# One ring of raw slots for single units and pairs, and three more panels with a second seven

## The chip, the cores and the metric

One NeuronCore of a Trainium2 chip runs the whole program. The metric is the device time of one execution in microseconds (us). Its engines work side by side, each on its own queue of instructions: PE (TensorE, matmuls), DVE (VectorE), ACT (ScalarE), POOL (GpSimd) and SP (SyncE, which here only issues transfers). Semaphores hold an instruction, and all that is queued behind it on its engine, until what it needs is there.

## The reference, cut to what matters

A decoder trunk of two layers on 256 tokens of width 2048, in float32. Layer 0 mixes tokens by gated linear attention, layer 1 by forgetting attention; both also attend to 256 memory tokens. Behind each stands a channel mixer, and only this is touched here:

```
def conv_ffn(h, w_up, conv_w, conv_b, w_down):
    u = causal_dwconv(h @ w_up, conv_w, conv_b)
    a, val = split_cols(u, [FFN_HIDDEN, FFN_HIDDEN])
    return (jax.nn.silu(a) * val) @ w_down
...
    h = rmsnorm(x, norm_ffn[i])
    x = x + conv_ffn(h, ffn_w_up[i], ffn_conv_w[i], ffn_conv_b[i], ffn_w_down[i])
```

`w_up` is 2048 x 11264 and `w_down` 5632 x 2048, so the weights are read once and used for 256 tokens. A causal convolution of width 3 along the tokens lies between.

## The kernel before, in words

**Precision.** TensorE multiplies in a rounded float32 form. Each float32 number is therefore carried in two parts, hi (rounded) and lo (what is left), and a product is made of three matmuls: hi x hi, lo x hi, hi x lo. Activations are split once. Weights are split as they arrive: ACT casts a raw tile to `whi` and DVE subtracts to get `wlo`. Both have five buffers.

**Units, panels, turns.** The weights lie in memory in the order of use, in units of at most 128 x 1024 numbers (512 KB). A panel is the units of one set of columns. `split_unit` (L211) loads one unit into a buffer `raw` (five buffers, tag "raw", on the right side of memory), casts and subtracts; `split_apart` (L195) does the same into smaller tiles. Ahead of the first mixer 20 panels of 8 units are loaded; a mixer has 264 units; between the mixers stand 7 panels of 8, 8 of 4 and 4 of 8 units.

**A channel mixer** (`ffn`, L1403) has 11 up panels of 16 units, numbered here 0 to 10, and three parts of down panels, of 16, 12 and 16 rows of blocks. The order is up panels 0 to 4, the two down panels of the first part, up panels 5 to 7, the two of the second, up panels 8 to 10, the third part (one panel of 16 joint units, then two of 8 narrow units). In code a panel is named by j, four times its number. `m` is a ring of 20 chunks of the gated product, which is why parts of down follow so early.

**Pairs and sevens** (`pair_steps`, L388). An up or joint down panel works on two halves of tokens by two halves of columns. A single unit k takes 4 places x 3 = 12 matmuls of 512 columns (L413). Two neighbouring units are a 2 x 2 block product; with sums of the two chunks of tokens at hand (`usum`, `dsum`) and sums of the two units of weights, seven block products do instead of eight: 21 matmuls instead of 24. This costs DVE four sums over half units (L438 to L441) in the raw tiles, and four casts and four subtractions (`split_more`, L376, instructions at L383 and L384): w1 and w2 of the raw units, w3 and w4 of the sums. The two units of a pair go to special tiles, `raw2`, two buffers in the pool that the mixer is given, and their loads (L432) are queued behind the last load issued. All up panels do this with units 6 and 7 (`SEVEN_UP`); panels in `MORE_IN` also with units 11 and 12 (`SEVEN_MORE`). In those panels the first pair comes after four single units, not six, three singles stand between the pairs, and five follow. The token sums for both pairs are made in every mixer (`input_sums`). Four of the joint down panels' pairs also go as sevens (`SEVEN_DOWN`).

**Order.** Instructions are ordered by a planner at build time: by priority (loads, casts and subtractions run ahead by `AHEAD`), by what they wait for, and by hand-written edges (`issue_after`). While a panel runs, the panel before is finished: its columns are turned by a trip through memory (L651, L656 on POOL), and taps, silu and gating are dealt out unit by unit (`tick`), in panels of `MORE_IN` with a larger share (1.7, not 1.45), and one unit earlier for the first half of the panel in front of one.

**The pools.** In layer 0 the mixer's pool is `turn1`. It is opened when the linear attention's pools `near` and `gla` close; in `near` lie the blocks (`blk`) that the norm ahead of the mixer sends through memory (`preparing`, L1596). In layer 1 the mixer's pool is `store`, opened when `turn2` closes, which holds only that norm's blocks. The block of the last 512 columns is sent (`far<-blk`) when the output projection `wo` in front of the mixer has ended. At the end of the first mixer the four blocks of the next norm are written: 0 and 1 in the `raw2` buffers, 2 and 3 in those of `dsum`.

Of the kernel before, what the change touches and what calls it, by code (L numbers as in the profile page):

```python
# [13 lines left out]
F32 = mybir.dt.float32  # L14
# [6 lines left out]
P = 128  # L21
# [13 lines left out]
SEVEN_UP = (6,)  # L35
SEVEN_DOWN = {4: 0, 10: 1, 20: 0, 34: 1}
SEVEN_MORE = 11
MORE_IN = (2, 5, 6, 8, 9)
SCRATCH = 4096


LEVELS = (64, 16, 4)
# [2 lines left out]
NUNIT = 1024  # L45
# [102 lines left out]
def _trunk(ctx: ExitStack, tc: tile.TileContext, xt, xtok, memt, wp, wgu, gns, gfin, cnv, par, msk, out):  # L148
    nc = tc.nc
    where, _ = _layout()  # L150
# [4 lines left out]
    rear = ctx.enter_context(tc.tile_pool(name="rear", bufs=1, side="right"))  # L155
# [28 lines left out]
            TE.matmul(warm, bufB[KC - 1][:, 0, :P], bufB[KC - 1], start=i == 0, stop=i == WARM - 1)  # L184

    loads, casts, lows, ends, last_mm, sent = [], [], [], [], [], []
    scratch = [sm]
    parked = []

# [5 lines left out]
    def split_apart(unit, spare):  # L195

        off, kcs, n = unit
        w = len(kcs) * n
        with tc.high_priority(offset=AHEAD):
            raw = rear.tile([P, NUNIT], F32, name="raw", tag="raw", bufs=5)  # L200
            loads.append(nc.sync.dma_start(raw[:, :w], wp[off : off + P * w].rearrange("(p n) -> p n", p=P)))
            hi, lo = [], []
            for j in range(len(kcs)):
                s = slice(j * n, (j + 1) * n)
                hi.append(spare())
                lo.append(spare())
                casts.append(S.activation(hi[j], raw[:, s], AF.Copy))
                lows.append(V.tensor_tensor(lo[j], raw[:, s], hi[j].bitcast(F32), ALU.subtract))
        return hi, lo

    def split_unit(unit, pieces=1, before=None, between=int):  # L211

        off, kcs, n = unit
        w = len(kcs) * n
        with tc.high_priority(offset=AHEAD):
            raw = rear.tile([P, NUNIT], F32, name="raw", tag="raw", bufs=5)
            hi = wpool.tile([P, NUNIT], F32R, name="whi", tag="whi", bufs=5)
            lo = wpool.tile([P, NUNIT], F32R, name="wlo", tag="wlo", bufs=5)
            src = wp[off : off + P * w].rearrange("(p n) -> p n", p=P)
            for i in range(pieces):  # L220
                s = slice(i * w // pieces, (i + 1) * w // pieces)
                if i:
                    between()
                loads.append(nc.sync.dma_start(raw[:, s], src[:, s]))
            if n % P:
                a, b, c = (t.rearrange("p (j m) -> p j m", j=len(kcs))[:, :, :n] for t in (raw[:, :w], hi, lo))
                casts.append(S.activation(b, a, AF.Copy))
                lows.append(V.tensor_tensor(c, a, b.bitcast(F32), ALU.subtract))
                return hi, lo
            for i in range(pieces):  # L230
                s = slice(i * w // pieces, (i + 1) * w // pieces)
                if before is not None:
                    before(i)
                casts.append(S.activation(hi[:, s], raw[:, s], AF.Copy))  # L234
                lows.append(V.tensor_tensor(lo[:, s], raw[:, s], hi[:, s].bitcast(F32), ALU.subtract))  # L235
        return hi, lo
# [150 lines left out]
    def pair_steps(units, src, sums, flip, pool, early, late, ahead=0):  # L387
# [38 lines left out]
        for k in plan:  # L426
            if k in sums:
                with tc.high_priority(offset=AHEAD):
                    ra, rb = [pool.tile([P, NUNIT], F32, name="raw2", tag="raw2", bufs=2) for _ in range(2)]
                    with tc.issue_after(loads[-1].ins):  # L430
                        for t, (off, _, w) in ((ra, units[k]), (rb, units[k + 1])):
                            loads.append(nc.sync.dma_start(t, wp[off : off + P * w].rearrange("(p n) -> p n", p=P)))  # L432
                st = [[sums[k][:, part, j, :] for part in range(2)] for j in (3, 0, 1, 2)]
                done = k == end[-1]
                w1 = split_more(ra[:, :512], 512)
                w2 = split_more(rb, 1024)
                with tc.high_priority(offset=AHEAD):
                    V.tensor_tensor(ra[:, :512], ra[:, 512:], ra[:, :512], ALU.subtract)  # L438
                    V.tensor_tensor(ra[:, 512:], rb[:, 512:], ra[:, 512:], ALU.subtract)  # L439
                    V.tensor_tensor(rb[:, 512:], rb[:, 512:], ra[:, :512], ALU.subtract)  # L440
                    summed = V.tensor_tensor(rb[:, :512], rb[:, :512], rb[:, 512:], ALU.subtract)  # L441
                three("p1", tok(k, 0), [t[:, :512] for t in w1], done)
                three("p2", tok(k + 1, 0), [t[:, :512] for t in w2])
                three("p3", st[3], [t[:, 512:] for t in w2])
                with tc.issue_after(summed.ins):
                    w3 = split_more(ra, 1024)
                three("p5", st[0], [t[:, :512] for t in w3], done)
                three("p7", st[2], [t[:, 512:] for t in w3], done)
                w4 = split_more(rb, 1024)
                three("p6", st[1], [t[:, 512:] for t in w4], done)  # L450
                last_mm.append(three("p4", tok(k + 1, 1), [t[:, :512] for t in w4]))
                if done:
                    with tc.issue_after(casts[-1].ins), tc.issue_after(lows[-1].ins):
                        early(bank)
                yield -1
                yield -1
                continue
            else:
                w = split_unit(units[k])
                last = k == n - 1  # L460
                steps = [(low, *place) for low in range(2) for place in places]
                if last:
                    steps.sort(key=lambda t: places.index(t[1:]))
                for low, name, b, h in steps:
                    for part in range(2 - low):
                        r = mm(name, tok(k, b)[part], w[low][:, h * 512 : (h + 1) * 512], last and low == 1)
                    if last and low:
                        ends.append(r)
                        late(b, h, bank[name])
                last_mm.append(r)  # L470
            yield k
# [923 lines left out]
    def ffn(l, nx, h, m, ys, zs, landing, then, pool, temps, last=None, spare=None):  # L1395
        with tc.tile_pool(name=f"ffn{l}", bufs=1) as fp:
            def held(name, i):
                return pool.tile([P, 2, 4, P], F32R, name=name, tag=f"{name}{i}")

            up_sums = {k: held("usum", k) for k in (*SEVEN_UP, SEVEN_MORE)}  # L1400
            rooms = {i: held("dsum", i) for i in range(2)}
            cw = fp.tile([P, 4 * 88], F32, name="cw")
            nc.sync.dma_start(cw, cnv[l])  # L1403
            taps = [fp.tile([P, 2, 2, T + i], F32, name=f"tap{i}") for i in range(3)]
# [89 lines left out]
            def up_pair(j):  # L1494

                count[2] += 1
                second = j // 4 in MORE_IN
                turns = [turn(j + 2 * h_, 7 if not h_ and j // 4 + 1 in MORE_IN else 8) for h_ in range(2)]
                u = {}
# [31 lines left out]
            def drive_up(j):  # L1531
                drive(up_pair(j), 1.7 if j // 4 in MORE_IN else 1.45)

# [27 lines left out]
            if l:  # L1561
                f2, f3 = [rows_tm(("down", l, p, f), src, evac) for f, evac in ((2, third), (3, last))]
            else:
                for f, k in ((2, 0), (3, 1)):
                    then.rooms[f] = lambda k=k: pool.tile([P, 4, 4, 2, 32], F32, name="tblk", tag=f"dsum{k}")
                f2 = panel_tm(("down", l, p, 2), src, third)
                f3 = panel_tm(("down", l, p, 3), src, lambda b, a: (add_to(3)(b, a), then(3, b)))
            last_pair = hi - lo - 4
# [9 lines left out]
            if l:  # L1578
                for u in range(3, 8):
                    f2(u)  # L1580
                for u in range(4):
                    f3(u)
                for b in range(2):
                    for u in range(4, 8):
                        f3(u, (b,), spare if u < 6 else None)
            else:
                hooks = {(2, 3): then.land, (2, 5): then.land, (2, 7): then.take, (3, 1): then.take, (3, 2): then.land,
                         (3, 5): then.take}
                for f, step, at in ((2, f2, 3), (3, f3, 0)):
                    for u in range(at, 8):  # L1590
                        step(u)
                        hooks.get((f, u), int)()

    def preparing(name, dst, pool, far, kept=None, tag="blk", queue=nc.sync):

# [43 lines left out]
    with tc.tile_pool(name="stash", bufs=1) as st:  # L1639
# [4 lines left out]
        with tc.tile_pool(name="turn1", bufs=1) as tp:  # L1644
            n2, then = preparing("kv", bufB, tp, dram, turned3, "raw2", nc.gpsimd)
# [13 lines left out]
    with tc.tile_pool(name="turn2", bufs=1) as tp:  # L1659
        n, then = preparing("ffn1", bufA, tp, dram)  # L1660
# [139 lines left out]
```

## Time and profile before

| | |
|---|---|
| median of 3 runs (lowest, highest) | 2210.38 us (2208.87, 2210.74) |
| the profiled execution | 2211.01 us |
| its span, first to last instruction | 2209.2 us |
| granted TensorE clock, mean | 0.998 |
| DVE, ACT busy | 82%, 65% of the span |
| read from memory | 469.62 MB |
| first mixer begins, second begins (first matmul of L413) | 456.9, 1493.7 us |

The page has the share of the span in which each engine was busy, the chain of work that ended last, and groups of instructions by line. In a row of a group stand line, engine, operation, output<-inputs and count; then busy time, mean ns of one, and what ended the engine's idle time in front of them. A row of the timeline has start, length, engine, line, operation, names and count, and in brackets the idle time in front of it and what released it.

### The profile page before, as it was taken

The numbers are of one execution on the slowest core, as the hardware profiler recorded it, in microseconds if no ns is written. First come the engines' busy times: TensorE is split into PE (matmuls) and PEld (weight loads), VectorE is DVE, ScalarE is ACT, GpSimd is POOL, SyncE is SP. The second block draws the span as 40 slices with busy tenths as digits, with TensorE's granted clock in tenths as the row PEclk, the third lists the DMA queues.
The fourth block names the chain that finished last, engine by engine and source line by source line (L and its number), as shares of the span: only waits on it lengthen the run. The fifth ranks groups of instructions, "written<-read, shape, count | busy, mean of one in ns | idle before, by whom it ended". The sixth has DMA issues, their size and how long they took to land.

```text
span 2209.2 us, 30105 instructions
## 1 busy us (share of the span) xinstructions
PE 2197.2 (99%) x10303; PEld 1849.1 (84%) x10303; DVE 1804.7 (82%) x2679; ACT 1426.7 (65%) x2268; POOL 137.2 (6%) x257
## 2 busy tenths in 40 slices
PE   9999999999999999999999999999999999999998
PEld 7888888888888888888888998888888888888886
DVE  7768976688998888889877669668898888888996
ACT  6655655556787568657865555455788657765774
POOL 0000000001100010001110000000100000100010
PEclk9999999999999999999999999999999999999999
DMA  9777677867778567666778767776677757676673
GB/s 367 253 223 220 192 209 225 256 219 249 235 248 267 189 212 248 229 232 221 247 252 259 227 201 244 228 240 231 227 239 236 254 184 247 228 266 206 223 271 131
DMA packets 166291, 515.42 MB, mean 233 GB/s; under 512 B 20780, under 2 KB 42552, under 8 KB 166136
## 3 DMA queue, kind: packets, MB, share of 16 engines
q1 hardware_dynamic: 149064, 460.99, 63.1%
q0 software_dynamic: 16496, 51.71, 7.4%
q8 instruction: 81, 1.33, 0.2%
q10 hardware_dynamic: 576, 0.79, 0.1%
q14 instruction: 74, 0.61, 0.1%
HBM read 469.62 MB, written 43.79 MB: 232 GB/s over the span
## 4 chain that ended last, share of the span: by engine, by line
PE 99%; DVE 0%; ACT 0%; issue 0%; DVEq 0%; ACTq 0%
PE acc L413 29%; PE acc L339 26%; PE ps_s L413 15%; PE ps_o L413 8%; PE ps_t L413 7%; PE acc L310 3%; PE acc L265 3%; PE ps_s L339 2%; PE acc L369 2%; PE acc L263 1%; PE ps_s L1036 0%; PE ps_o L702 0%; PE ps_s L702 0%; PE ps_s L1309 0%; PE ps_s L1082 0%; PE ps_o L1264 0%
## 5 line engine op out<-in xcount | busy, mean ns | idle before, releaser
L235 DVE TENSOR_TENSOR wlo<-raw,whi 128x1024 fp32r<-128x1024 f32 (+2 forms) x697 | 828.0, 1201 | 235.3 <-ACT whi L234 214.4
L234 ACT ACTIVATE whi<-raw 128x1024 fp32r<-128x1024 f32 (+2 forms) x697 | 717.6, 1046 | 356.1 <-PE acc L339 135.2
L339 PE MATMUL acc<-whi,B 128*128 128x512 f32 (+3 forms) x1248 | 290.9, 369 | 0.0
L383 ACT ACTIVATE whi<-raw 128x1024 fp32r<-128x1024 f32 (+1 forms) x160 | 151.9, 954 | 197.1 <-DVE raw L439 64.5
L339 PEld LDWEIGHTS acc<-whi,B 128*128 128x128 f32 x1248 | 226.8, 188 | 28.1
L384 DVE TENSOR_TENSOR wlo<-raw,whi 128x1024 fp32r<-128x1024 f32 (+1 forms) x160 | 173.4, 1085 | 25.9 <-ACT whi L383 23.5
L413 PE MATMUL acc<-whi,mix 128*128 128x512 f32 x750 | 191.9, 389 | 0.0
L413 PE MATMUL acc<-whi,B 128*128 128x512 f32 x728 | 188.4, 389 | 0.0
L413 PEld LDWEIGHTS acc<-whi,mix 128*128 128x128 f32 x750 | 140.8, 188 | 29.3
L413 PEld LDWEIGHTS acc<-whi,B 128*128 128x128 f32 x728 | 136.6, 188 | 28.4
L339 PE MATMUL acc<-wlo,B 128*128 128x512 f32 (+3 forms) x624 | 159.1, 369 | 0.0
L339 PEld LDWEIGHTS acc<-wlo,B 128*128 128x128 f32 x624 | 114.2, 188 | 14.6
L1415 ACT ACTIVATE tap<-yzu,cw 128x256 f32<-128x256 f32 x264 | 121.2, 534 | 2.6 <-DVE wlo L235 1.9
L1415 ACT ACTIVATE tap<-fvt,cw 128x256 f32<-128x256 f32 x264 | 121.2, 534 | 0.3 <-DMA fvt<-far 0.3
L1422 DVE TENSOR_TENSOR tap<-tap,tap 128x1024 f32<-128x1024 f32 x88 | 106.7, 1213 | 5.9 <-ACT tap L1415 5.9
L413 PE MATMUL acc<-wlo,mix 128*128 128x512 f32 x375 | 105.6, 389 | 0.0
L413 PE MATMUL ps_s<-whi,mix 128*128 128x512 f32 x382 | 105.1, 389 | 0.0
L413 PE MATMUL acc<-wlo,B 128*128 128x512 f32 x364 | 104.6, 389 | 0.0
L413 PE MATMUL ps_s<-whi,B 128*128 128x512 f32 x336 | 92.1, 389 | 0.0
L413 PEld LDWEIGHTS ps_s<-whi,mix 128*128 128x128 f32 x382 | 71.7, 188 | 14.9
L413 PEld LDWEIGHTS acc<-wlo,mix 128*128 128x128 f32 x375 | 70.4, 188 | 14.6
L413 PEld LDWEIGHTS acc<-wlo,B 128*128 128x128 f32 x364 | 68.3, 188 | 14.2
(502 smaller groups left out, 3890.2 us busy)
## 6 DMA issues: line engine op xcount, KB each, us to landing
raw<-wp SPq DMA_DIRECT2D x741, 512.0 KB, 4.7
fvt<-far POOLq DMA_DIRECT2D x100, 128.0 KB, 3.9
raw<-wp SPq DMA_DIRECT2D x32, 384.0 KB, 3.5
far<-yu POOLq DMA_DIRECT2D x22, 512.0 KB, 3.7
far<-yzu POOLq DMA_DIRECT2D x22, 512.0 KB, 4.3
yzu<-far POOLq DMA_DIRECT2D x88, 128.0 KB, 4.3
raw<-wp SPq DMA_DIRECT2D x24, 388.0 KB, 3.7
x<-xtok SPq DMA_DIRECT2D x8, 512.0 KB, 7.3
```

The source lines that it names most:

```text
L234: casts.append(S.activation(hi[:, s], raw[:, s], AF.Copy))
L235: lows.append(V.tensor_tensor(lo[:, s], raw[:, s], hi[:, s].bitcast(F32), ALU.subtract))
L263: mm = TE.matmul(acc[p][c][:, :T], w[:, s], both[:, 0, :], start=False, stop=end and j == 3)
L265: mm = TE.matmul(acc[p][c], w[:, s], both, start=u == j == 0, stop=end and j == 3)
L310: mm = TE.matmul(acc[b][:, :n], src[kcs[j] - base][:, part, b * P : (b + 1) * P], w, start=u == 0 and low == part == j == 0, stop=u == end ...
L339: mm = TE.matmul(acc[b][:, :n], src[kc - base][:, part, b * P : (b + 1) * P], ready[low][:, j * room : j * room + n], start=i == low == pa ...
L369: mm = TE.matmul(acc[b][:, :n], src[kc - base][:, part, b * P : (b + 1) * P], w, start=i == low == part == j == 0, stop=i == end and low = ...
L383: casts.append(S.activation(hi[:, :n], src, AF.Copy))
L384: lows.append(V.tensor_tensor(lo[:, :n], src, hi[:, :n].bitcast(F32), ALU.subtract))
L413: r = TE.matmul(bank[name], x, w, start=name not in begun, stop=last)
L1415: S.activation(by_run(taps[i][:, s, c, i:]), zs[slot][:, :, 2 * c + s], AF.Copy if i else AF.Identity, bias=0.0 if i else w[3], scale=w[2 ...
L1422: V.tensor_tensor(taps[0], taps[0], taps[n][:, :, :, :T], ALU.add)
```

## The change: one ring, and MORE_IN of eight panels

The five raw buffers become one tile `home`, cut into five slots; `raw_slot()` counts its calls in `taken` and returns slot number `taken % len(slots)`. While a mixer runs, a tile `guest` in the mixer's pool adds two slots, numbers 5 and 6, so that seven are turned; at the mixer's end they are taken off again. Both units of a pair take slots of this ring, in turn with the single units. `MORE_IN` grows from five panels to eight (1, 7 and 10 are new). The four blocks at the end of the first mixer go to the buffers of the two `usum` and the two `dsum`.

```
-MORE_IN = (2, 5, 6, 8, 9)
+MORE_IN = (1, 2, 5, 6, 7, 8, 9, 10)
+RAWS = 5
...
+    home = rear.tile([P, RAWS * NUNIT], F32, name="raw")
+    slots, taken = [home[:, i * NUNIT : (i + 1) * NUNIT] for i in range(RAWS)], [0]
+
+    def raw_slot():
+
+        taken[0] += 1
+        return slots[taken[0] % len(slots)]
...
-            raw = rear.tile([P, NUNIT], F32, name="raw", tag="raw", bufs=5)
+            raw = raw_slot()
...
-                    ra, rb = [pool.tile([P, NUNIT], F32, name="raw2", tag="raw2", bufs=2) for _ in range(2)]
+                    ra, rb = raw_slot(), raw_slot()
...
             rooms = {i: held("dsum", i) for i in range(2)}
+            guest = pool.tile([P, 2 * NUNIT], F32, name="raw2")
+            slots.extend(guest[:, i * NUNIT : (i + 1) * NUNIT] for i in range(2))
...
-                for f, k in ((2, 0), (3, 1)):
-                    then.rooms[f] = lambda k=k: pool.tile([P, 4, 4, 2, 32], F32, name="tblk", tag=f"dsum{k}")
+                for f, tag in enumerate((f"usum{SEVEN_UP[0]}", f"usum{SEVEN_MORE}", "dsum0", "dsum1")):
+                    then.rooms[f] = lambda tag=tag: pool.tile([P, 4, 4, 2, 32], F32, name="tblk", tag=tag)
...
+            del slots[RAWS:]
```

The line with `raw_slot()` stands twice, in `split_apart` and in `split_unit`.

More of the change, by code (lines that the diff above doesn't have):

```diff
@@ L215, in split_unit @@
         with tc.high_priority(offset=AHEAD):
-            raw = rear.tile([P, NUNIT], F32, name="raw", tag="raw", bufs=5)
+            raw = raw_slot()
             hi = wpool.tile([P, NUNIT], F32R, name="whi", tag="whi", bufs=5)
```

## The prediction

> **What bounds the kernel now.** I read the page first: span, busy shares, the chain that ended last.
>
> ```profile
> span 2209.2 us, 30105 instructions
> PE 2197.2 (99%) x10303; PEld 1849.1 (84%) x10303; DVE 1804.7 (82%) x2679; ACT 1426.7 (65%) x2268; POOL 137.2 (6%) x257
> PE 99%; DVE 0%; ACT 0%; issue 0%; DVEq 0%; ACTq 0%
> ```
>
> TensorE is the chain, from end to end. So each matmul that goes is worth its spacing, and each new wait of TensorE is paid in full; DVE, at 82%, is paid only where it hands a weight over late. The timeline of PE in an up panel gives the spacing:
>
> ```profile
> 801.21 1.98 PE L413 MATMUL acc<-whi,B 128*128 128x512 f32 x8
> 803.02 1.07 PE L413 MATMUL acc<-wlo,B 128*128 128x512 f32 x4
> 803.93 1.98 PE L413 MATMUL acc<-whi,B 128*128 128x512 f32 x8
> ```
>
> Twelve matmuls, a single unit, run from 801.21 to 803.93: 2.72 us, 0.2267 us each.
>
> The sum is made against the profiled execution, 2211.0 us (span 2209.2 and 1.8 around it); the median of the runs, 2210.4, lies 0.6 under it. This kernel's measurement tells about 0.2% (4.4 us) from no change.
>
> **The matmuls that go: -4.1 us.** A pair in the long form takes 2 x 12 = 24 matmuls, as a seven 7 x 3 = 21. Three more panels in each of two mixers save 2 x 3 x 3 = 18 matmuls: 18 x 0.2267 = 4.1 us. No operation is added to TensorE. Bytes from memory stay the same.
>
> **DVE's share of a new pair.** Its price, by the groups of lines:
>
> ```profile
> L235 DVE TENSOR_TENSOR wlo<-raw,whi 128x1024 fp32r<-128x1024 f32 (+2 forms) x697 | 828.0, 1201 | 235.3 <-ACT whi L234 214.4 <-PE acc L339 5.1 <-issue 3.1
> L384 DVE TENSOR_TENSOR wlo<-raw,whi 128x1024 fp32r<-128x1024 f32 (+1 forms) x160 | 173.4, 1085 | 25.9 <-ACT whi L383 23.5
> L441 DVE TENSOR_TENSOR raw<-raw 128x512 f32<-128x512 f32 x40 | 27.6, 691 | 1.0
> L438 DVE TENSOR_TENSOR raw<-raw 128x512 f32<-128x512 f32 x40 | 27.2, 681 | 0.6
> ```
>
> A seven costs DVE 173.4 / 40 = 4.34 us of subtractions and four weight sums (L438 to L441) of 0.68 to 0.69, 2.74: 7.08 us. Two singles cost 2 x 1.20 = 2.40. So each new pair adds 4.68 us to DVE while TensorE's panel gets 0.68 shorter. Is there room? Windows on panels 1, 2, 7, 10 and the last joint down panel of the first mixer (start:end, length, then PE, PEld, DVE, ACT, POOL busy):
>
> ```profile
> 499.60:542.50 42.90, 42.90 (x191) 35.50 (x190) 35.09 (x41) 33.40 (x53) 5.47 (x10) 1.00 0.77 261
> 542.50:584.70 42.20, 42.20 (x187) 34.80 (x186) 38.91 (x45) 29.76 (x46) 5.49 (x10) 1.00 0.66 202
> 840.40:883.30 42.90, 42.90 (x191) 35.51 (x190) 36.53 (x47) 34.03 (x56) 5.52 (x10) 1.00 0.75 244
> 1032.20:1075.00 42.80, 42.80 (x190) 35.45 (x189) 36.46 (x47) 33.97 (x56) 5.49 (x10) 1.00 0.76 252
> 1075.00:1118.00 43.00, 42.71 (x189) 35.02 (x188) 41.78 (x51) 30.89 (x50) 5.50 (x10) 1.00 0.73 238
> ```
>
> DVE would be busy 39.8 of 42.2 in panel 1, 41.2 of 42.2 in panel 7, 41.1 of 42.1 in panel 10. It fits on the mean, with a microsecond over. What can be lost is local: panel 2 and the down panel take over a smaller lead. In panel 2's second pair the last cast and its matmul already stand 0.08 us apart:
>
> ```profile
> 554.93 1.61 SPq L432 DMA_DIRECT2D raw<-wp  x2
> 563.82 1.06 ACT L383 ACTIVATE whi<-raw 128x1024 fp32r<-128x1024 f32 x1 [2.10 <-DMA raw<-wp]
> 568.31 1.06 ACT L383 ACTIVATE whi<-raw 128x1024 fp32r<-128x1024 f32 x1 [0.39 <-PE acc L413]
> 569.45 0.71 PE L413 MATMUL ps_t<-whi,usum 128*128 128x512 f32 x2
> ```
>
> The same rows show what the ring repairs: this pair's loads left only at 554.93, when the first pair gave back the two special tiles, and ACT waited 2.10 us for them. With seven slots turned in one ring the second pair's slots are those of the units two and three places ahead of the first pair, so that wait goes. Against it: panel 1 leaves 4.68 + 0.68 = 5.4 us less lead, of which about half its 7.8 idle us (3.9) takes up its part and the vanished wait 2.1. Bounds per mixer: nothing lost, or one whole 4.68. I take 1.5 (about 0.5 at panel 2, 1.0 at the down panel behind panel 10, where DVE has 1.2 us free), since the idle rows lie nearer to the lower end: **+3.0** for both, bounds 0 and 9.4. TensorE has no wait in these panels that could be won back.
>
> **The start of each mixer, where the ring reaches the guest tile: the large term.** Before, the first six singles use the five old slots; the two special tiles are first touched by the pair of unit 6. The pool they lie in takes over memory of a pool that closes just then, the one with the norm's blocks (near, then turn2). SP and ACT at both starts:
>
> ```profile
> 461.47 0.33 SPq L651 DMA_DIRECT2D far<-blk  x1
> 466.26 0.80 SPq L432 DMA_DIRECT2D raw<-wp  x2
> 1498.23 1.10 SPq L651 DMA_DIRECT2D far<-blk  x1
> 1504.01 0.80 SPq L432 DMA_DIRECT2D raw<-wp  x2
> 1504.07 0.63 ACT L688 ACTIVATE usum<-cv 128x512 fp32r<-128x512 f32 x1 [1.90 <-DMA far<-blk]
> 469.55 0.63 ACT L383 ACTIVATE whi<-raw 128x512 fp32r<-128x512 f32 x1 [2.57 <-DMA raw<-wp]
> 471.08 1.06 ACT L383 ACTIVATE whi<-raw 128x1024 fp32r<-128x1024 f32 x1 [0.90 <-DMA raw<-wp]
> ```
>
> Twice the first load into the special tiles leaves at the moment at which the last block's transfer has landed (ACT's write to usum, a tile of the same pool, names that transfer). The guest is allocated in the same pool; I take it that its first write waits for the same thing. Now count calls of the ring. Ahead of the first mixer: 20 panels of 8 units, 160. The mixer: 264. Between: 7 panels of 8, 8 of 4, 4 of 8, 120. So the second mixer begins with call 545, and 545 mod 7 = 6: **its very first unit goes into the guest's second half.** The first mixer begins with call 161, slot 0; its unit 5 and the pair's first half get slots 5 and 6.
>
> *Second mixer.* Unit 0's load now leaves at 1504.0. From issue to landing the first pair's took 469.55 - 466.26 = 3.3 us; the cast takes 1.06: hi is ready at 1508.4. TensorE wants it here:
>
> ```profile
> 1493.66 1.07 PE L413 MATMUL acc<-whi,mix 128*128 128x512 f32 x4
> 1514.08 0.74 PE L413 MATMUL ps_t<-whi,usum 128*128 128x512 f32 x2 [0.94 <-ACT whi L383]
> ```
>
> That is a stall of 14.7 us. Unit 0 opens the accumulators, so nothing of the mixer can go ahead of it; wo is done. Behind the waiting load stand, on SP, the pair's loads and the returns of the norm's blocks; on ACT and DVE the casts of units 1 to 5, whose loads use the five old slots and can have landed: all of that runs faster than TensorE's 2.72 us a unit, and the pair's old stall of 0.94 disappears in the gained lead. Net **+13.8**. Bounds: 0 if the guest's memory is free earlier, 14.7 if nothing is won back.
>
> TensorE then restarts from idle. What that costs, by the kernel's first matmuls, and the granted clock behind its last ones (0.62 is the last but two columns):
>
> ```profile
> 1.46 3.36 PE L184 MATMUL ps_o<-B 128*128 128x512 f32 x7 [1.46 <-DVE B L181]
> 4.71 2.08 PE L310 MATMUL acc<-whi,A 128*128 128x512 f32 x4
> 6.58 1.02 PE L310 MATMUL acc<-wlo,A 128*128 128x512 f32 x2
> 7.43 1.09 PE L310 MATMUL acc<-whi,A 128*128 128x512 f32 x4
> 2200.00:2209.00 9.00, 0.23 (x1) 0.00 (x0) 3.50 (x12) 1.83 (x6) 0.00 (x0) 0.62 0.58 185
> ```
>
> Thirteen matmuls took 7.43 - 1.46 = 5.97 us instead of 2.95, and within 9 us of the end the clock had fallen to a mean of 0.62. So a stop of 14.7 us should cost a second ramp: **+3.0**, bounds 0 and 3.0. The Trainium skill (TensorE: Matmul & The Clock Gate, Part 1) has the array fall to half rate after an idle window of about 3.4 us and come back after as long a busy one; at half rate that would lose an estimated 1.7 us, and the sum would be 1.3 lower. The ramp in these rows, 5.97 us, is longer than that.
>
> *First mixer.* Call 161 gets the slot of call 160, but unit 0 is wanted only at 470.50 - 5 x 2.72 = 456.9. DVE lets go of unit 160 here:
>
> ```profile
> 443.69 1.22 DVE L235 TENSOR_TENSOR wlo<-raw,whi 128x1024 fp32r<-128x1024 f32 x1 [0.88 <-ACT whi L234]
> 470.50 1.98 PE L413 MATMUL acc<-whi,B 128*128 128x512 f32 x8
> 475.04 1.06 ACT L383 ACTIVATE whi<-raw 128x1024 fp32r<-128x1024 f32 x1 [1.52 <-PE acc L413]
> 476.17 0.72 PE L413 MATMUL ps_t<-whi,usum 128*128 128x512 f32 x2
> ```
>
> 444.9 + 3.3 + 1.06 = 449.3: hidden with 7.6 us over; without that cover it would cost the 4.4. Unit 5 leaves at 466.3 and is cast by 470.6, where TensorE wants it at 470.50; the pair's loads fall one place back, 471.08 - 469.55 = 1.5 us, and its last cast stands 0.07 us ahead of its matmul. So about **+1.6**, bounds 0 and 2.5.
>
> **What costs nothing.** The first layer's norm blocks 0 and 1 move from the special tiles to the input sums' tiles: those are read last by panel 10's pair, one down panel (43 us) earlier; were that gone, a DVE transpose would wait. The earlier taps and the larger share in front of and in the new panels move the same instructions by one unit; POOL's transfers keep their places. Leaving a mixer, the ring's next slot is that of five calls back (calls 425 and 420), as before.
>
> **Sum:** -4.1 + 3.0 + 13.8 + 3.0 + 1.6 = +17.3. 2211.0 + 17.3 = 2228.3, less 0.6 for the median: **2228 us**, slower.
>
> **Rivals.**
> *The guest is free in time* (not slower). For it: the new pool is larger than the one that it follows, and its guest may lie on other memory than the blocks. Against: two tiles of that pool, usum and the special ones, both waited. Then only -4.1 + 3.0 is left: 2209.9, by the median 2209, within 0.2%; it decides if the guest may be written before about 1488. With nothing lost in the panels it is 2206.3.
> *DVE becomes the bound*: the 4.68 us of panels 1 and 10 are lost whole, at panel 2 and at the down panel, in both mixers, on top of the starts: 2211.0 - 4.1 + 18.4 + 18.7 = 2244. For it: 0.08 us of lead there. Against: 3.3 idle us in panel 2's window.
> *The slots are not told apart*, as they are now parts of one tile: each load would wait for the unit before, 4.7 us (the page's landing) + 1.05 + 1.20 = 6.95 a unit, 808 units, 5,600 us. Against: the taps' tiles are already written in parts.
>
> **Chances.** Forecast 0.85 (two tiles in two places against one argument); guest free 0.10; DVE bound 0.03; not told apart 0.02. The range takes the forecast's terms from their low ends (clock, panels and first mixer at nothing: 2220.7; 4 us less if the last block leaves earlier) to their high ends (panels 9.4: 2234.7, and one more unit late): 2216 to 2238, some 8 in 10. Faster 0.03 and same 0.07 are the free guest's; slower 0.90.
>
> **What would show it.** Right: 5814 matmuls on L413; PE idle of about 15 us at 1494, its first L413 whi late, released by ACT, ACT by a load; the guest's first load behind far<-blk; matmul spacing of 0.45 for some microseconds behind it. In panel 2 ACT no longer waits 2 us for the second pair. Wrong: unit 0 of the second mixer loaded before 1488, or PE waits in panels 2, 7 and 10 of more than 5 us a mixer.

## The result, and the profile after

The changed kernel takes 2220.79 us (median of 5 runs, 2219.84 to 2221.95); the kernel before took 2210.52 beside it (5 runs, 2208.87 to 2210.86). The ratio is 1.0048, with a 95% interval of 1.0033 to 1.0062: slower by 10.3 us, inside the range and 7.2 us under the forecast of 2228. The profiled execution took 2219.84 us, 8.8 more than that of before, so its trace shows 8.8 of the 10.3 us.

In the new kernel the lines have moved down: the matmul of the mixers is L421 (it was L413), that of `wo` L347 (L339), the cast of a single unit L242 (L234), the casts and subtractions of a pair L391 and L392, a single unit's load L232, a pair's L440, `far<-blk` L659. The page, in the lines that were shown of before (span, busy time, the chain), and one of its groups:

```profile
span 2218.0 us, 30190 instructions
PE 2196.9 (99%) x10285; PEld 1846.7 (83%) x10285; DVE 1828.6 (82%) x2715; ACT 1437.8 (65%) x2280; POOL 136.8 (6%) x257
PE 96%; DVE 2%; ACT 1%; DMA 1%; issue 0%; SPq 0%; DVEq 0%; ACTq 0%
L421 PE MATMUL acc<-whi,mix 128*128 128x512 f32 x746 | 191.7, 392 | 8.7 <-ACT whi L242 8.7
```

TensorE has 18 matmuls fewer (10285 for 10303), and the chain that ended last, wholly TensorE's before, now runs for a few per cent through other engines and a DMA. The last line names the place: one group of matmuls waited 8.7 us for the cast of a single unit. The chain of waits, in order of time (start, length, what), shows what that cast waited for:

```profile
1479.83 12.48 PE acc L347 x55
...
1493.77 0.62 DVE x L507
...
1494.42 0.72 DVE blk L1637
...
1495.16 2.57 DMA far<-blk
1497.73 0.02 SPq L232
...
1497.78 3.42 DMA raw<-wp
...
1501.28 1.06 ACT whi L242
...
1502.39 19.11 PE acc L421 x72
```

Read it downwards: `wo` ends, its last block is added to x and transposed, the block goes to memory, and only when that transfer has landed does the load of the mixer's unit 0 leave, at 1497.78. The timeline of PE at that place, with the standstill in brackets:

```profile
1502.39 3.78 PE L421 MATMUL acc<-whi,mix 128*128 128x512 f32 x8 [8.73 <-ACT whi L242]
1505.97 1.89 PE L421 MATMUL acc<-wlo,mix 128*128 128x512 f32 x4
1507.68 2.03 PE L421 MATMUL acc<-whi,mix 128*128 128x512 f32 x8
1509.55 1.07 PE L421 MATMUL acc<-wlo,mix 128*128 128x512 f32 x4
```

After the stop of 8.73 us twelve matmuls take 1507.68 - 1502.39 = 5.29 us, where 2.72 is the usual; from 1507.68 on the usual pace is back. The granted clock, the last figure but two in the row of a window, was 0.50 from shortly after TensorE stopped until then, and 1.00 on both sides of it:

```profile
1497.50:1507.70 10.20, 5.31 (x13) 4.15 (x14) 6.02 (x6) 7.05 (x11) 0.00 (x0) 0.50 0.56 184
```

The account of the 8.99 us by which the last matmul starts later (2199.84 before, 2208.83 after), all from the starts of TensorE's matmuls (the stop of 8.73 us is counted from the end of the last matmul, so it is a little more here):

| | predicted | measured |
|---|---|---|
| 18 matmuls that go | -4.1 | -4.08 |
| first mixer, its first pair | +1.6 | +1.58 |
| new pairs, panels 7 and 10 of the first mixer, 2, 7 and 10 of the second (the pair in panel 2 had lost 0.11 before) | +3.0 | +1.67 - 0.11 |
| from the end of the first mixer to the start of the second | +14.7 | +8.90 |
| slow matmuls behind that stop | +3.0 | +2.63 |
| the old stall of the second mixer's first pair | -0.94 | -1.34 |
| ahead of the first mixer | none | -0.24 |
| sum | +17.3 | +9.0 |

The predicted worry about DVE is answered by the same windows as before (DVE's busy time is the third figure that has a count behind it), on panels 1, 2, 7, 10 and the last joint down panel of the first mixer:

```profile
501.20:543.40 42.20, 42.20 (x188) 34.95 (x187) 39.23 (x49) 35.37 (x56) 5.45 (x10) 1.00 0.74 247
543.40:585.50 42.10, 42.10 (x187) 34.87 (x186) 39.98 (x49) 32.22 (x50) 5.47 (x10) 1.00 0.71 233
841.20:883.70 42.50, 42.46 (x187) 34.84 (x186) 42.08 (x54) 33.48 (x54) 5.50 (x10) 1.00 0.77 248
1032.60:1075.10 42.50, 42.50 (x188) 34.86 (x187) 42.14 (x54) 34.14 (x56) 5.51 (x10) 1.00 0.75 244
1075.10:1118.20 43.10, 42.81 (x189) 35.14 (x188) 40.30 (x50) 32.34 (x53) 5.49 (x10) 1.00 0.83 257
```

DVE is busy 42.1 of 42.5 us in panels 7 and 10, and TensorE loses only 0.29 to 0.37 us in each of them.

### The profile page after: what moved, and what is told of

Same layout as the page of the kernel before. It is cut to its first block, busy times and chain, and to the rows that moved or that the text cites. A ratio compares the mean times of both kernels' runs of the same rounds, so it can differ in the third digit from the quotient of the medians.

```text
span 2218.0 us, 30190 instructions
## 1 busy us (share of the span) xinstructions
PE 2196.9 (99%) x10285; PEld 1846.7 (83%) x10285; DVE 1828.6 (82%) x2715; ACT 1437.8 (65%) x2280; POOL 136.8 (6%) x257
## 3 DMA queue, kind: packets, MB, share of 16 engines
q8 instruction: 80, 1.31, 0.2%
## 4 chain that ended last, share of the span: by engine, by line
PE 96%; DVE 2%; ACT 1%; DMA 1%; issue 0%; SPq 0%; DVEq 0%; ACTq 0%
PE acc L421 29%; PE acc L347 26%; PE ps_s L421 15%; PE ps_o L421 7%; PE ps_t L421 7%; PE acc L273 3%; PE acc L318 3%; PE ps_s L347 2%; PE acc L377 2%; PE acc L271 1%; PE ps_s L1044 0%; DMA raw<-wp 0%; ACT whi L242 0%; PE ps_o L710 0%; PE ps_s L710 0%
## 5 line engine op out<-in xcount | busy, mean ns | idle before, releaser
L243 DVE TENSOR_TENSOR wlo<-raw,whi 128x1024 fp32r<-128x1024 f32 (+2 forms) x685 | 812.5, 1200 | 222.9 <-ACT whi L242 200.8
L242 ACT ACTIVATE whi<-raw 128x1024 fp32r<-128x1024 f32 (+2 forms) x685 | 704.3, 1045 | 347.8 <-PE acc L347 131.2
L347 PE MATMUL acc<-whi,B 128*128 128x512 f32 (+3 forms) x1248 | 290.9, 369 | 0.0
L391 ACT ACTIVATE whi<-raw 128x1024 fp32r<-128x1024 f32 (+1 forms) x184 | 173.7, 953 | 179.4 <-DVE raw L447 65.7
L347 PEld LDWEIGHTS acc<-whi,B 128*128 128x128 f32 x1248 | 226.8, 188 | 28.1
L392 DVE TENSOR_TENSOR wlo<-raw,whi 128x1024 fp32r<-128x1024 f32 (+1 forms) x184 | 198.3, 1084 | 26.8 <-ACT whi L391 23.8
L421 PE MATMUL acc<-whi,mix 128*128 128x512 f32 x746 | 191.7, 392 | 8.7 <-ACT whi L242 8.7
L421 PE MATMUL acc<-whi,B 128*128 128x512 f32 x720 | 186.9, 389 | 0.0
L421 PEld LDWEIGHTS acc<-whi,mix 128*128 128x128 f32 x746 | 141.2, 189 | 38.7 <-ACT whi L242 9.2
L347 PE MATMUL acc<-wlo,B 128*128 128x512 f32 (+3 forms) x624 | 159.1, 369 | 0.0
L421 PEld LDWEIGHTS acc<-whi,B 128*128 128x128 f32 x720 | 135.1, 188 | 28.5 <-ACT whi L242 0.5
L347 PEld LDWEIGHTS acc<-wlo,B 128*128 128x128 f32 x624 | 114.2, 188 | 14.6
L421 PE MATMUL acc<-wlo,mix 128*128 128x512 f32 x373 | 105.0, 392 | 0.0
L421 PE MATMUL acc<-wlo,B 128*128 128x512 f32 x360 | 103.8, 389 | 0.0
L421 PE MATMUL ps_s<-whi,mix 128*128 128x512 f32 x374 | 103.8, 389 | 0.0
L421 PE MATMUL ps_s<-whi,B 128*128 128x512 f32 x324 | 89.9, 389 | 0.0
L421 PEld LDWEIGHTS acc<-wlo,mix 128*128 128x128 f32 x373 | 70.6, 189 | 14.8
L421 PEld LDWEIGHTS ps_s<-whi,mix 128*128 128x128 f32 x374 | 70.2, 188 | 14.6
L421 PEld LDWEIGHTS acc<-wlo,B 128*128 128x128 f32 x360 | 67.6, 188 | 14.0
```

The source lines that it names most:

```text
L347: mm = TE.matmul(acc[b][:, :n], src[kc - base][:, part, b * P : (b + 1) * P], ready[low][:, j * room : j * room + n], start=i == low == pa ...
L391: casts.append(S.activation(hi[:, :n], src, AF.Copy))
L392: lows.append(V.tensor_tensor(lo[:, :n], src, hi[:, :n].bitcast(F32), ALU.subtract))
L421: r = TE.matmul(bank[name], x, w, start=name not in begun, stop=last)
```

## The experiments

The theory: all that is lost in earnest comes from the guest. Its slots come free late, because the first write into them waits for the norm's last block, and the ring's count happens to hand one of them to the second mixer's very first unit. The rivals: the eight sevens themselves are too dear (DVE, lead), or the ring is.

**Where in the turn the guest's slots come.** The slots are put in an order, oldest first, with the guest's two at the end, and the count is set so that the mixer's first unit takes the oldest:

```
+            at = (taken[0] + 1) % len(slots)
+            slots[:] = slots[at:] + slots[:at]
+            taken[0] = -1
             slots.extend(guest[:, i * NUNIT : (i + 1) * NUNIT] for i in range(2))
...
             del slots[RAWS:]
+            taken[0] = -1
```

> Only the turn of the ring is changed: each mixer begins with the old slots, oldest first, so that the guest's slots come sixth and seventh (unit 5 and the pair's first half) in the second mixer too. Theory A (the guest's first write waits for the norm's last block, and what waits behind it costs): the stop of 8.73 us before the second mixer and the slow matmuls behind it (2.6 us) go; a stop of 1 to 3 us at the first pair takes their place, as in the first mixer, where 1.6 us are lost. Time 2211 +- 1.5 us. Theory B (the 24 added sums and the DVE work of the new pairs cost it, or the ring itself): the time stays at 2219 to 2222.

Measured: 2212.25 us (2210.49 to 2213.19), ratio 1.0008 (0.9999 to 1.0017) to the kernel before. The stop is gone, the second mixer starts at 1493.75, and 8.5 us are won back. What is left stands in panel 0, 2.14 us in the first mixer and 4.14 in the second, more than the 1 to 3 that were expected. The second mixer's, on PE and then on SP:

```profile
1508.26 2.11 PE L421 MATMUL acc<-whi,mix 128*128 128x512 f32 x8 [0.75 <-ACT whi L242]
...
1513.15 0.73 PE L421 MATMUL acc<-whi,mix 128*128 128x512 f32 x2 [1.19 <-ACT whi L391]
...
1517.01 0.73 PE L421 MATMUL ps_t<-whi,usum 128*128 128x512 f32 x2 [1.25 <-ACT whi L391]
```

```profile
1498.32 0.33 SPq L659 DMA_DIRECT2D far<-blk  x1
...
1503.57 0.33 SPq L232 DMA_DIRECT2D raw<-wp  x1
```

The guest's first load still leaves only behind `far<-blk`, now for unit 5, and that transfer takes 1503.57 - 1498.32 = 5.25 us, not 2.57. The wait has been moved to where it is mostly covered, not removed.

**The same slots at the third and fourth turn of the second mixer.** As above, but put in at place 2 there; in the first mixer they stay last.

> As the run with the guest sixth and seventh, but in the second mixer the guest's slots come third and fourth (units 2 and 3), in the first sixth and seventh. Theory A with the wait as the only cause: the load of unit 2 leaves at the same moment, and TensorE has two units (5.44 us) to do first; the stop before the second mixer goes, one of 8.7 - 5.4 = 3.3 us (3 to 5) stands at unit 2. Time 2213 to 2216, between the changed kernel and the run with the guest sixth and seventh. If what costs is any use of the guest early in the mixer and not its place, the time stays at 2220.

Measured: 2214.76 us (2213.63 to 2216.36), ratio 1.0021 (1.0012 to 1.0030). On PE:

```profile
1499.22 0.39 PE L421 MATMUL acc<-wlo,mix 128*128 128x512 f32 x1
1503.02 3.78 PE L421 MATMUL acc<-whi,mix 128*128 128x512 f32 x8 [3.42 <-ACT whi L242]
1506.61 1.91 PE L421 MATMUL acc<-wlo,mix 128*128 128x512 f32 x4
1508.31 2.45 PE L421 MATMUL acc<-whi,mix 128*128 128x512 f32 x8
```

Two units of work cover 5.4 us of the wait, and 3.42 are left, at unit 2. With the guest's slot first, third and sixth in the turn, TensorE stands 8.73, 3.42 and 0.75 us: the stop follows the place. A surprise lies in the rows behind it: 3.42 us of standstill cost a ramp no shorter than that behind 8.73. By windows:

```profile
1499.61:1502.40 2.79, 0.00 (x0) 0.00 (x0) 0.07 (x1) 0.48 (x1) 0.00 (x0) 1.00 0.98 349
1503.02:1509.16 6.14, 6.14 (x14) 4.80 (x15) 6.12 (x9) 6.00 (x9) 0.00 (x0) 0.50 0.76 213
```

The first of them begins where the last matmul ends, still at a clock of 1.00; then fourteen matmuls run at 0.50 and take 6.14 us for 3.17. The forecast had no ramp in it, so that its time was met with some luck.

**Is it the pool?** The guest is allocated from `fp`, the pool that `ffn` itself opens (for the taps, among others), instead of `turn1` or `store`:

```
-            guest = pool.tile([P, 2 * NUNIT], F32, name="raw2")
+            guest = fp.tile([P, 2 * NUNIT], F32, name="raw2")
```

> Only the pool of the guest tile is changed: the mixer's own pool (that of the taps) in place of the one that follows the norm's. The turn of the ring stays, so unit 0 of the second mixer is still in the guest. Theory A: the first write no longer waits for the norm's last block, neither mixer stops at its start beyond what the input sums cost; the stop of 8.73 us, the ramp of 2.6 and the 1.6 of the first mixer go. What is left is -4.1 us of matmuls and about 1.6 us of small stops in panels 2, 7 and 10: 2206 to 2208 us, faster than the kernel before. Theory B: 2219 to 2222.

Measured: 2206.24 us (2205.78 to 2206.77), ratio 0.9982 (0.9973 to 0.9991): faster than both kernels, by 4.1 us than before and 14.6 than the change. Every unit takes the same slot as in the change; only the tile's place in memory differs, and with it what its first write waits for. On PE and on SP:

```profile
1491.71 0.62 PE L347 MATMUL acc<-wlo,B 128*128 128x512 f32 x2
1492.16 1.07 PE L421 MATMUL acc<-whi,mix 128*128 128x512 f32 x4
```

```profile
1481.91 1.86 SPq L440 DMA_DIRECT2D raw<-wp  x2
...
1496.73 0.33 SPq L659 DMA_DIRECT2D far<-blk  x1
```

The mixer's matmuls follow those of `wo` at the usual 0.45 us for two, without a stop. The first pair's loads now leave 15 us ahead of the block that they were bound to follow, and panel 0 loses nothing in either mixer. What is left of the sevens' price is 0.35 + 0.29 us in panels 7 and 10 of the first mixer and 0.37 + 0.30 of the second: 1.31 us against 4.08 of matmuls.

**Is the slow stretch behind the stop due to the standstill?** The change, and in front of the second mixer 36 matmuls that put nothing into the result, in the time in which TensorE stands:

```
+            if l:
+                warm = work("o")
+                with tc.issue_after(ends[-1].ins):
+                    for i in range(36):
+                        TE.matmul(warm, onesr, m[0], start=i == 0, stop=i == 35)
```

> The changed kernel with 36 matmuls more, of no use to the result, between the last matmul of wo and the second mixer: 36 x 0.2267 = 8.2 us, put into the stop of 8.73. Theory C (the slow matmuls behind the stop come of TensorE having stood still): spacing 0.2267 from unit 0's first matmul on, and 2.6 us less, 2218. If the spacing of 0.427 has another cause (the weights just arrived, memory ports): 2221, or a little above where the matmuls reach over the stop.

Measured: 2218.34 us (2216.55 to 2218.71), ratio 1.0037 (1.0024 to 1.0050); 2.45 us less than the change by the medians, 1.4 by the spans (in this version the first mixer's panel 0 loses 3.4 us, not 1.7, and the second mixer starts 1.2 us later). On PE, and the window of unit 0's matmuls:

```profile
1494.73 8.32 PE L1550 MATMUL ps_o<-mix,onesr 128*128 128x512 f32 x36
1503.60 2.14 PE L421 MATMUL acc<-whi,mix 128*128 128x512 f32 x8 [0.55 <-ACT whi L242]
1505.58 1.08 PE L421 MATMUL acc<-wlo,mix 128*128 128x512 f32 x4
1506.49 1.98 PE L421 MATMUL acc<-whi,mix 128*128 128x512 f32 x8
```

```profile
1503.60:1506.49 2.89, 2.89 (x12) 2.36 (x13) 2.89 (x3) 2.89 (x4) 0.00 (x0) 1.00 0.16 34
```

Unit 0 comes as late behind `wo` as in the change, but its twelve matmuls now take 1506.49 - 1503.60 = 2.89 us, at a granted clock of 1.00. Of the 2.6 us that they lost, 0.2 are left: the slow stretch is the standstill's, and not that of late weights.

**The ring without the new sevens.** The change with `MORE_IN = (2, 5, 6, 8, 9)`.

> The change without the three new sevens: MORE_IN is that of before, the ring stays. Theory A: the start of the second mixer stops as in the changed kernel; 18 matmuls come back (+4.1) and the stops of panels 2, 7, 10 (1.6) go: 2223 +- 1.5 us, slower than the whole change. Theory B with the sevens as the cost: 2210 to 2212.

Measured: 2223.57 us (2221.00 to 2224.70), ratio 1.0059 (1.0046 to 1.0071). On PE:

```profile
1506.00 3.54 PE L421 MATMUL acc<-whi,mix 128*128 128x512 f32 x8 [8.75 <-ACT whi L242]
1509.38 1.08 PE L421 MATMUL acc<-wlo,mix 128*128 128x512 f32 x4
```

The ring alone carries the whole stop; the new sevens win 2.8 us of it back. Here eight matmuls are slow, 3.38 us for 1.81, so the ramp isn't always of one length. That the forecast of 2223 was met is partly luck: the ramp is 1.0 us cheaper than in the change, and the first mixer's panel 0 loses 3.9 us, 2.3 more.

**The ring without the new sevens and without the stop.** The version with the guest from `fp`, and the old five panels:

> The changed kernel with the guest tile in the pool fp, which is free long before the mixer, and with the old five panels in MORE_IN: the ring alone, without its stop. Theory (with a free guest the ring costs nothing at the start of either mixer, and the sevens are worth their matmuls less what panels 7 and 10 were seen to lose, 4.08 - 1.31 = 2.8 us): 2206.2 + 2.8 = 2209 us, between 2208 and 2210; the second mixer starts without a stop, its first pair without the old 1.3 us, no wait over 0.2 us in any up panel. Rival (the planner's other order makes the first pair late, as with the ring alone and the guest in the mixer's pool, where panel 0 of the first mixer lost 4 us): 2211 to 2214, with the waits in panel 0.

Measured: 2209.01 us (2208.50 to 2209.31), ratio 0.9992 (0.9983 to 1.0001). The theory's 2209 holds: the new sevens are worth 2209.01 - 2206.24 = 2.77 us, their matmuls less what panels 7 and 10 lose. The ring itself, beside the old five panels, gives 1.2 to 1.8 us by the medians, which the interval doesn't tell from nothing; in the trace the old stall of the second mixer's first pair (1.34 us) is gone.

**The sevens without the ring.** The kernel before with `MORE_IN = (1, 2, 5, 6, 7, 8, 9, 10)`.

> The kernel before with MORE_IN of eight panels, and the separate buffers for pairs as before. Theory A: no stop at the second mixer's start; -4.1 us of matmuls, and the panels with new pairs lose 1.6 us or more, since the second pair's loads wait for the first pair's tiles: 2208 to 2212 us. Theory B with the sevens as the cost: 2219 to 2222. If the ring is worth nothing beside the sevens, 2208.

Measured: 2229.91 us (2225.95 to 2230.94), ratio 1.0086 (1.0072 to 1.0100). A miss by 18 us: without the ring the new sevens cost 19.5 us, with it (and a free guest) they win 2.8. Panels 2, 7 and 10 of the two mixers lose 1.22 and 1.64, 3.94 and 3.88, 5.66 and 4.39 us, 20.7 in all. Another 3.2 us go in the second mixer at the pair of the second down panel behind panel 7, whose casts stand on ACT behind taps and wait for DVE's sums, not for a load. Panel 10 of the first mixer, on SP, on ACT and on PE:

```profile
1049.18 1.67 SPq L432 DMA_DIRECT2D raw<-wp  x2
```

```profile
1056.84 0.63 ACT L383 ACTIVATE whi<-raw 128x512 fp32r<-128x512 f32 x1 [4.81 <-DMA raw<-wp]
1057.89 4.77 ACT L1415 ACTIVATE tap<-fvt,cw 128x256 f32<-128x256 f32 x11
```

```profile
1057.52 0.72 PE L413 MATMUL ps_o<-whi,B 128*128 128x512 f32 x2 [1.64 <-ACT whi L383]
...
1063.66 0.73 PE L413 MATMUL acc<-whi,B 128*128 128x512 f32 x2 [1.53 <-ACT whi L383]
...
1067.55 0.73 PE L413 MATMUL ps_t<-whi,usum 128*128 128x512 f32 x2 [1.27 <-ACT whi L383]
```

The second pair's loads leave at 1049.18, when the first pair has given back the two special tiles; ACT waits 4.81 us for them, and eleven taps stand behind that wait and in front of the pair's next casts. By the list of waits ACT waits for loads of pairs 20.4 us here against 7.7 in the kernel before, and the version with the free guest has no such wait in its list. In the change's own panel 2 the prediction's sign of it is seen too: the second pair's casts, which waited 2.10 us for a load before, wait for no load.

**Would another division of the seven tiles have done it?** The sevens without the ring once more, with three tiles for single units and four for pairs (and the norm's four blocks placed as in the change):

```
-            raw = rear.tile([P, NUNIT], F32, name="raw", tag="raw", bufs=5)
+            raw = rear.tile([P, NUNIT], F32, name="raw", tag="raw", bufs=3)
...
-                    ra, rb = [pool.tile([P, NUNIT], F32, name="raw2", tag="raw2", bufs=2) for _ in range(2)]
+                    ra, rb = [pool.tile([P, NUNIT], F32, name="raw2", tag="raw2", bufs=4) for _ in range(2)]
```

> The kernel before with eight panels in MORE_IN and its seven tiles divided otherwise: three for single units, four (not two) for pairs, so that a pair's loads needn't wait for the former pair; no ring. It asks what made the eight panels so dear without the ring. Theory (the two special tiles tie a pair's loads to the former pair): the waits of ACT for the loads of a second pair go, and the time is 2205 to 2212 us, 18 to 25 under the eight panels with two special tiles. Rival 1 (the single units need their five tiles: a tile is busy 3.3 to 4.7 us of load, 1.06 of cast and 1.20 of subtraction, 5.6 to 7.0 us, and three of them give 3 x 2.72 = 8.2): where loads come later than 5.9 us TensorE waits, in single panels all over the kernel, and the time is over 2215. Rival 2 (it is DVE's work that makes the eight panels dear): 2230 as before, with the waits in panels 2, 7 and 10.

Measured: 2303.63 us (2298.08 to 2308.39), ratio 1.0418 (1.0403 to 1.0433). The first rival holds: single units starve. ACT's waits for their loads (total us, times, longest):

```profile
ACT whi L234 <- DMA raw<-wp: 334.0, 222, 7.2
```

In the change the same wait is 22.0 us in 18 times. The longest wait for a pair's load is 2.9 us here, down from 4.8, but with single units late everywhere this run can't tell what the two tied tiles alone had cost. What it does show is that pairs can't be given two more tiles out of the five without loss; the ring gives both the use of all seven.

**Are more sevens to be had?** The version with the guest from `fp`, with `MORE_IN` of ten panels, 1 to 10:

> The guest in the taps' pool, and a second seven in panels 3 and 4 too, ten of eleven. Four sevens more save 12 matmuls, 2.7 us. DVE had 37.4 us of 42.8 in panel 3 and 38.9 of 42.9 in panel 4; with 4.68 each 42.1 and 43.6 of 42.2, and panels 1 and 2 in front have used up the lead (0.04 us at panel 2's first pair). Theory D (DVE is the bound from here on): panels 3 and 4 lose 2 to 4 us a mixer, 2208 to 2212 in all. If the lead rebuilds at once: 2203.5.

Measured: 2211.51 us (2210.19 to 2212.25), ratio 1.0006 (0.9997 to 1.0015): 5.3 us slower than with eight panels. Panels 3 and 4 lose 1.10 and 2.71 us in the first mixer, 1.22 and 2.48 in the second, 7.5 in all, for 12 matmuls less, 2.7 us. Their windows in the first mixer:

```profile
583.80:627.00 43.20, 42.69 (x187) 34.74 (x186) 41.95 (x55) 34.58 (x57) 5.49 (x10) 1.00 0.71 240
627.00:670.00 43.00, 41.22 (x179) 33.05 (x179) 41.26 (x54) 32.88 (x53) 5.46 (x10) 1.00 0.67 232
```

In these two DVE is asked for 41 to 42 us, behind two panels that have a second pair too, and TensorE waits (41.22 busy of 43.00): in panel 4's second pair the last cast waits 0.86 us for one of DVE's sums, and TensorE 0.73 for that cast. The rival in which DVE becomes the bound begins here, two panels further than the change goes.

## Why the prediction was right, and where its sizes were off

**Right in mechanism.** The matmuls that go (-4.08 for -4.1), the first mixer's pair (+1.58 for +1.6), the guest in the second mixer's unit 0, bound to the norm's last block, and the ramp behind the stop were all found where they were put. That the change's loss is the guest's is shown: one word, the pool from which the tile comes, takes 14.6 us away. Two steps of that are settled by runs that change one thing each, the place in the turn (8.73, 3.42 and 0.75 us of standstill) and the ramp (the 36 matmuls). That 1.58 us lies so near to 1.6 is partly luck: with the slots in the same turn, the first mixer's panel 0 lost 3.4 us in the version with the 36 matmuls and 3.9 with the ring alone.

**Mis-sized: the stop, 14.7 predicted, 8.73 measured.** The step that failed is "unit 0's load now leaves at 1504.0": it took over the landing of `far<-blk` from the trace of before, though the change itself moves it (the low end of the range allowed 4 us for a block that leaves earlier). Two things were late in that trace, and both go when the mixer's first unit waits. DVE, before and after:

```profile
1492.47 1.13 DVE L545 SCALAR_TENSOR_TENSOR mix<-yzu,gains,mix 128x128 fp32r<-128x128 f32 x4
1497.50 0.70 DVE L1626 STREAM_TRANSPOSE blk<-x 128x512 f32<-128x512 f32 x1
```

```profile
1492.34 0.69 DVE L507 TENSOR_TENSOR x<-x,acc 128x512 f32<-128x512 f32 x1 [6.75 <-PE acc L347]
1494.42 0.71 DVE L1637 STREAM_TRANSPOSE blk<-x 128x512 f32<-128x512 f32 x1
```

The transpose of the last block starts 3.08 us earlier, behind additions for which DVE stood ready (6.75 us idle) where before it still had the mixer's work in hand. And the transfer, 1498.23 to 1504.01 (5.8 us) before, takes 2.57. SP after:

```profile
1482.39 0.85 SPq L232 DMA_DIRECT2D raw<-wp  x2
1495.16 0.33 SPq L659 DMA_DIRECT2D far<-blk  x1
1497.78 0.33 SPq L232 DMA_DIRECT2D raw<-wp  x1
```

No load was sent in the 12 us ahead of the transfer; where a load of weights had been sent just ahead of it, it took 5.8 us (before) and 5.25 (guest last). Seven more traces agree: 2.57 to 2.58 us in the other three versions in which no load was under way (guest third, the 36 matmuls, the ring alone), and 5.0 to 6.2 in four with one (guest from `fp` with five, eight and ten panels, the sevens without the ring). That the load is what lengthens it was not tried by itself. So unit 0's load leaves 6.2 us earlier than predicted; of that 0.1 goes again in the load (3.42 for 3.3) and as much in the small steps between, and the stop is 6.0 us shorter.

**Mis-sized: the ramp, 3.0 predicted, 2.63 measured.** The kernel's first matmuls were a fair price. That it is TensorE's clock is seen in the windows: 0.50 granted in the slow stretches, 1.00 where the 36 matmuls fill the gap. The Trainium skill (TensorE: Matmul & The Clock Gate, Part 1) has the array run at half rate until a window of about 3.4 us has been busy; here twelve matmuls run at 0.44 us each over 5.29 us, with the ring alone eight over 3.38 us, and with the guest third fourteen over 6.14 us. The Trainium skill also has that window free-running (the same section), and the traces agree: the low clock lasted from 1497.5 to 1507.7 in the change, from 1502.4 to 1509.2 with the guest third and from 1502.3 to 1509.1 with the ring alone, 10.2, 6.8 and 6.8 us, which is three and two times 3.4. What a stop costs thus depends on where in such a window TensorE starts again. By the prediction's estimate of 1.7 us, worked out from the Trainium skill, the term would have been 0.9 too small. The other half of the Trainium skill's rule, that an idle window of about 3.4 us loses the rate, asks for more than was needed here: with the guest third the clock fell 2.8 us after the last matmul's end (1499.61 to 1502.4), and the stop of 3.42 us cost a full ramp.

**Mis-sized: the panels, 3.0 predicted, 1.67 measured,** and in another place: not in the down panel behind panel 10 but within panels 7, 10 and (second mixer) 2. DVE's added work was about right (42.1 us in panels 7 and 10, where 41.2 and 41.1 were expected), and the reason given for the small price, that the ring takes the second pair's wait away, turns out to be worth far more than the 2.1 us put down for it. Without the ring the same sevens cost 19.5 us. (By the count of calls the second pair's slots are those of the units one and two places ahead of the first pair, not two and three; the loads are early either way.)

**The rivals.** A guest that is free in time would give 2209 or, with nothing lost in the panels, 2206.3: the version with the guest from `fp` took 2206.24. That it meets the second of these is luck: the panels do lose 1.31 us, and the old stall of the second mixer's first pair, which that sum left in place, gives 1.34 back. The condition of the rival didn't hold in the change. DVE as the bound needs ten panels. The slots are told apart: each load waits for its own slot, or the time would be thousands of us longer.

**Open.** The trace shows that the guest's first write waits for the block's transfer, and a run that it doesn't when the tile comes from another pool. Whether it waits because it lies on that block's own memory, or because the whole pool is held until all accesses to the closed one are over, was not tried. In its pool four tiles, 16 KB a partition together, are allocated ahead of it, and the norm's pool has 16 KB, which would speak for the second if both pools began at the same place and were filled in the order of allocation; where the tiles lie was not read, so that is an argument, not a measurement.

## What to carry to other kernels

When a ring of slots gets more places, count which piece of work meets the new place first, and ask when its memory comes free: the best place for it is memory that has long been free, the second best is last in the turn. A wait that a change puts in moves other work too, so the landing time on which it depends has to be worked out again with the engines and queues that fall idle; taken from the trace of before it was 6.2 us too late here. Slots in one ring are worth most where two users would otherwise be tied to their own few: it was worth 1 to 2 us beside five such panels and 23.7 beside eight (2229.91 to 2206.24), since a late load holds up everything that is queued behind its cast.

## What the runs showed of the hardware

A standstill of TensorE of 8.73 us was followed by twelve slow matmuls, 5.29 us for 2.72, one of 3.42 us by fourteen, 6.14 us for 3.17, and one of 8.75 us in another version by eight, 3.38 us for 1.81. The granted clock in these stretches was 0.50, and matmuls of no use in the gap removed them.

The low clock came in stretches of 3.4, 6.8 and 10.2 us. It didn't take a period without matmuls to bring it on: in the version with three and four tiles it fell at 884.4 us, though TensorE had been busy for 1.74 of the 3.41 us before. Nor did it end at once: with the guest third TensorE was busy for 2.8 us of the period from 1502.4 to 1505.8, and the clock stayed at 0.50 for another period, whereas 3.1 us of a period were enough with the ring alone (1506.0 to 1509.1).

One block's transfer to memory took 2.57 to 2.58 us in four traces when no load was under way and 5.0 to 6.2 us in six others beside a load of weights.
